# Turning the memory's P on VectorE and moving it through DRAM, with a new order in GpSimd's queue

## The chip, the cores and the metric

The kernel runs on one core of a Trainium2 chip. The metric is the device time of one execution in microseconds; the median of three runs is given. A profile of one execution shows each engine's instructions (PE = TensorE, with PEld for its weight loads, DVE = VectorE, ACT = ScalarE, POOL = GpSimd, SP = SyncE) and the DMA traffic.

## The reference, cut to what matters

Two layers of a hybrid decoder trunk: sequence 256, model width 1024, all in f32.

```python
for l in range(2):
    h = rms_norm(x, norm_g[l])
    q_a, k_a, v_a, q_h, f_h, i_h, q_m, z = split(h @ w_in[l], 512-wide columns)   # z is 1536 wide
    o_a = causal softmax attention, 8 heads x 64 (256 keys are one block: only the own block counts)
    o_h = rms_norm(hgrn2 recurrence, 4 heads x 128)
    km, vm = split(rms_norm(mem, mem_norm_g[l]) @ w_mem_kv[l])                     # 256 memory tokens
    p   = softmax(norm(q_m) @ norm(km).T * 128**-0.5)                              # 4 heads x 128
    o_m = p @ vm
    y = concat(o_a, o_h, o_m) * silu(z)
    x = x + y @ w_out[l]
```

The softmax weights p of the memory attention are "the memory's P" below; those of the causal attention are "the first P" (heads 0 to 3) and "the second P" (heads 4 to 7). The gated output of the recurrence, before it is turned, is "zh".

## The kernel before, in words

**Weights in chunks.** PE is fed by weights of 128 x 1024 f32 (512 KB). For each layer 60 chunks pass in order: 8 of w_mem_kv, 40 of w_in (four for each 512-wide group of columns, the last four groups being QM, VA, ZA, ZM), and 12 of w_out. Each matmul product is made from split operands: a high half (`wh`, made by ACT at L186 or L189) and the rest (`wl`, by DVE at L198 or L201), and three matmuls for each product. SP loads the raw chunk (`wr`, four buffers, L161); there are three buffers each for `wh` and `wl`. A chunk's high half is traced three chunks ahead of its use, the low half two, the load five.

**Generators.** Everything else (norms, attention, the recurrence) is written as generators. `slot()` is called twice for each chunk (L231), and each call lets every active generator go one step; `yield n` waits n steps. `st["c"]` counts the chunks done. `done` holds names that generators wait for. This fixes the order in which instructions are traced. A scheduler then orders each engine's instructions by its own simulation of time, so an instruction that it holds to be ready can overtake an earlier one. `tc.keep_in_program_order(ins)` ties an instruction behind the one traced just before it on the same engine; `mm_row` is a matmul tied in this way; `tc.issue_after(ins)` ties what is issued in its block behind `ins` on that engine.

**Turning a tile.** To turn a 128-row tile there are two ways. On PE: transposes against `ident` into PSUM, then copies to SBUF. Or `across` (L88): DVE transposes 32 x 32 blocks into `blk` (L95), one DMA writes `blk` to the DRAM tile `there` (L103), and four DMAs, one for each strip of 32 rows, read it back in the turned order (L108). `kn` and `kr` go this way on SP's queue; the first P, the second P and zh go this way on GpSimd's queue. `there` has two buffers.

**The end of a layer.** In time order: the first P is turned (into the tile `PT`), the memory's queries are turned on PE (L1068), the memory's scores (L1087 ff.), their softmax (L1100 to L1118), the transposes of the memory's P on PE (L1128, eight for each of two units, with two copies on ACT and two subtractions on DVE into the two halves of the tile `mP`), then P·V of the first P (L1015, L1016) and of the memory (L1142). Then comes w_out (L1164), which takes its 12 row blocks in the order recurrence, causal attention, memory (`KT_ORDER`). Its first four blocks need zh turned and split (`unstripped`, L122: `yh` by ACT at L125, `yl` by DVE at L126); the branch outputs of the attentions are split in `y_store` (L742). zh is sent on its way after the second P has been turned by DVE (`y_turned`, L752).

Of the kernel before, what the change touches and what calls it, by code (L numbers as in the profile page):

```python
# [3 lines left out]

# [8 lines left out]
F32 = mybir.dt.float32  # L13
F32R = mybir.dt.float32r
# [4 lines left out]
OP = mybir.AluOpType  # L19
# [26 lines left out]
def hymba_kernel(ctx: ExitStack, tc: tile.TileContext, x, mem, mem_t, positions, w_in, w_out, w_mem_kv,  # L46
                 gains, moba_g, out):
    nc = tc.nc
    cst = ctx.enter_context(tc.tile_pool(name="cst", bufs=1))
    sb = ctx.enter_context(tc.tile_pool(name="sb", bufs=1))  # L50
    psum = ctx.enter_context(tc.tile_pool(name="psum", bufs=1, space=PS))
    away = ctx.enter_context(tc.tile_pool(name="away", bufs=1, space=bass.MemoryType.DRAM))
# [8 lines left out]
    held = {"sd": 0, "P": 0, "PTh": 0, "PTl": 0, "blk": 0}  # L61
    room_of = {"sd": 4, "P": 2, "PTh": 1, "PTl": 1, "blk": 1}

    def room(what, n=1):
        while held[what] + n > room_of[what]:
            yield
# [9 lines left out]
    def side_tile():  # L76
        held["sd"] += 1
        assert held["sd"] <= 4
        return psum.tile([128, 512], F32, name="sd", tag="sd", bufs=4)

    def rel(what="sd", n=1):
        held[what] -= n
# [2 lines left out]
        return sb.tile([128, n], F32, name=name, tag=name, bufs=2)  # L85


    def across(dst, src, n, stage=None, free=None, name=None, q=None):  # L88
        q = q or nc.sync
        if stage is None:  # L90
            yield from room("blk")
            held["blk"] += 1
        tag = stage or "blk"
        blk = sb.tile([128, 4, n * 32], F32, name="blk", tag=tag, bufs=1)
        nc.vector.transpose(blk.rearrange("p c (n i) -> p c n i", n=n),  # L95
                            src.rearrange("p (n c i) -> p c n i", n=n, c=4))
        if free is not None:
            rel(free)
        if name is not None:
            done.add(name)  # L100
        yield 2
        there = away.tile([4, 32, 4, n * 32], F32, name="there", tag="there", bufs=2)
        q.dma_start(there.rearrange("q j c r -> (q j) c r"), blk)  # L103
        if stage is None:
            rel("blk")
        yield 4
        for c in range(4):
            q.dma_start(dst[c * 32:c * 32 + 32], there[:, :, c].rearrange("q j r -> j q r"))  # L108
            if c == 1:
                yield  # L110

    def turned(a, stage=None, q=None):
        yield from across(a.rearrange("p (q r) -> p q r", q=4), a, 8, stage, q=q)
        yield 5

    def strips(a):
# [2 lines left out]
    def strip_of(o, t):  # L119
        return o[:, :, t * 128:(t + 1) * 128].rearrange("p h (q i) -> p h q i", q=4)  # L120

    def unstripped(oh, ol, a):  # L122
        for t in range(2):
            src, to = strips(a)[:, :, t], strip_of(oh, t)
            nc.scalar.copy(to, src)  # L125
            nc.vector.tensor_tensor(strip_of(ol, t), src, to.bitcast(F32), op=OP.subtract)  # L126

    chunks = []

# [28 lines left out]
    st = {"dma": 0, "h": 0, "l": 0, "c": 0}  # L158
# [51 lines left out]
    T = {}  # L210

    def step():
        for e in list(active):
            e[0] -= 1
            if e[0] <= 0:
                try:
                    e[0] = next(e[1]) or 1
                except StopIteration:
                    active.remove(e)
# [11 lines left out]
    def slot(first):  # L231
        if first:
            c = st["c"]
            dma_to(c + 1 + DMA_AHEAD)
            h_to(c + 1 + H_AHEAD)
            l_to(c + 1 + L_AHEAD)
        step()

    def mm(o, a, b, s, e):
        nc.tensor.matmul(o, lhsT=a, rhs=b, start=s, stop=e)  # L240
# [347 lines left out]
    def heads(t, n):  # L588
        return t.rearrange("p (h d) -> p h d", h=n)
# [161 lines left out]

    def y_turned(l):  # L752
        flat = zh.rearrange("p t s -> p (t s)")
        while f"turned1{l}" not in done:
            yield
        yield from turned(flat, "hq0", nc.gpsimd)
        unstripped(*y_tiles(H_), flat)
        yield
        for k in range(4):
            done.add(f"y{4 * H_ + k}_{l}")  # L760
# [213 lines left out]
    def g_moba_unit(l, u, P, mx):  # L974
        rq, nr = T["rq"], T["nr"]
        nb = small("nba%d" % u, 8)
        sm = small("sma%d" % u, 8)
        ri = small("ria%d" % u, 8)
        if u:
            yield from room("sd", 2)  # L980
            ps = second(u)
            yield
            second_masked(u, ps, P, mx)
        nc.vector.tensor_tensor(nb.rearrange("p (t h) -> p t h", t=2), mx.rearrange("p (t h) -> p t h", t=2),  # L984
                                nr.rearrange("p (t h) -> p t h", t=2)[:, :, 4 * u:4 * u + 4], op=OP.mult)
        yield
        for t in range(2):
            for i in range(4):
                c, r = t * 4 + i, t * 8 + 4 * u + i
                nc.scalar.activation(P[:, i, kc[t]], P[:, i, kc[t]], AF.Exp, bias=nb[:, c:c + 1],  # L990
                                     scale=rq[:, r:r + 1], accum_out=sm[:, c:c + 1])
            yield
        yield
        nc.vector.reciprocal(ri, sm)
        for t in range(2):
            for i in range(4):
                c = t * 4 + i
                nc.vector.tensor_scalar(P[:, i, kc[t]], P[:, i, kc[t]], ri[:, c:c + 1], None, op0=OP.mult)
        yield 2
        tag = ("PTh", "PTl")[u]  # L1000
        yield from take(tag)
        PT = sb.tile([128, 4, 384], F32, name="PT", tag=tag, bufs=1)
        yield from across(PT, P.rearrange("p i s -> p (i s)"), 12, free="P", name=f"turned{u}{l}", q=nc.gpsimd)
        yield 13
        while f"va{l}" not in done or f"z{A_}{l}" not in done:
            yield
        va = T["va"]
        yield from room("sd")
        po = side_tile()
        for i in range(4):  # L1010
            h = 4 * u + i
            rows, c = slice(64 * (i % 2), 64 * (i % 2) + 64), (i // 2) * 256
            pieces = PT.rearrange("p q (n s) -> p n q s", n=12)[:, 3 * i:3 * i + 3]
            o = po[rows, c:c + 256].rearrange("p (b q s) -> p b q s", b=2, q=4)
            (mm if i else mm_row)(o, va[:, 0, h * 64:(h + 1) * 64], pieces[:, 0:2], True, False)  # L1015
            mm(o[:, 1], va[:, 1, h * 64:(h + 1) * 64], pieces[:, 2], False, True)  # L1016
        rel(tag)
        yield
        y_store(l, A_, u, po)
# [58 lines left out]
    def g_mem_unit(l, u, qm, r, nr):  # L1078
# [36 lines left out]
        for t in range(2):  # L1115
            for i in range(2):
                c = 2 * t + i
                nc.vector.tensor_scalar(P[:, t, i], P[:, t, i], ri[:, c:c + 1], None, op0=OP.mult)  # L1118
        yield 5
        while f"scores1{l}" not in done:  # L1120
            yield
        PT = [sb.tile([128, 2, 2, 256], F32R, name="mP", tag=n, bufs=1) for n in (("hF", "kmh"), ("ih", "kml"))[u]]
        for b in range(2):
            yield from room("sd")
            pt = side_tile()
            for i in range(2):
                for t in range(2):
                    nc.tensor.transpose(pt[:, i * 256 + t * 128:i * 256 + (t + 1) * 128],  # L1128
                                        P[:, t, i, b * 128:(b + 1) * 128], ident)
            nc.scalar.copy(PT[0][:, b], heads(pt, 2))  # L1130
            nc.vector.tensor_tensor(PT[1][:, b], heads(pt, 2), PT[0][:, b].bitcast(F32), op=OP.subtract)
            rel()
        if u == 0:
            rel("P")
        yield 8
        yield from room("sd")
        po = side_tile()
        for i in range(2):
            hs = slice((2 * u + i) * 128, (2 * u + i + 1) * 128)
            for b in range(2):  # L1140
                for x, y in passes:
                    (mm if i or b or x != passes[0][0] or y != passes[0][1] else mm_row)(po[:, i * 256:(i + 1) * 256], vm[x][:, b, hs], PT[y][:, b, i],  # L1142
                       b == 0 and (x, y) == passes[0], b == 1 and (x, y) == passes[2])
        yield
        while f"z{M_}{l}" not in done:
            yield
        y_store(l, M_, u, po)
# [2 lines left out]
    def w_out_phase(l):  # L1150
# [6 lines left out]
        def part(i, n, kt, t, cols=(0, 1), o=0, w=512, pinned=False, to=None):  # L1157
            br, k = divmod(kt, 4)
            yh, yl = (a[:, k, t * 128:(t + 1) * 128] for a in T[f"y{br}"])
            for c in cols:  # L1160
                cs = slice(c * 512 + o, c * 512 + o + w)
                a = acc[t][c][:, o:o + w] if to is None else to[:, :w]
                for j, (y, wt) in enumerate(((yh, whs[i]), (yh, wls[i]), (yl, whs[i]))):
                    ins = nc.tensor.matmul(a, lhsT=y, rhs=wt[:, cs], start=n == (0 if to is None else nk - 2) and j == 0,  # L1164
                                           stop=n == nk - 1 and j == 2)
                    if pinned:
                        tc.keep_in_program_order(ins)

        def fin():
# [108 lines left out]
```

## Time and profile before

| | |
|---|---|
| median of 3 runs | 397.27 us (395.93, 397.27, 397.28) |
| the profiled execution's own time | 399.69 us |
| its span in the profile | 397.9 us |
| PE busy | 390.5 us, 2871 matmuls |
| DVE, ACT, POOL busy | 314.6, 251.1, 70.3 us |
| bytes moved by DMA | 80.33 MB, 202 GB/s over the span |
| of these on GpSimd's queue | 8.39 MB |

The span is the time between the first and the last instruction in the profile; the execution's own time has a little more around it. The chain that ended last is followed back from the last instruction, at each step to what released it. A windows view gives each engine's busy time in a stretch of the span, the TensorE clock that was granted (1.00 is full) and the mean busy share of the 16 DMA engines. Layer 0's last stretch lies at about 128 to 198 us, layer 1's at about 320 to 394 us.

### The profile page before, as it was taken

Reading aid. Unit: us, or ns where it says so; the run is one execution under the profiler, and the core shown is the slowest. Engines: PE = TensorE matmul, PEld = TensorE weight load, DVE = VectorE, ACT = ScalarE, POOL = GpSimd, SP = SyncE. Lnnn points to the kernel's source line nnn. Section 1 sums busy time; section 2 is a strip of 40 time slices with the busy share of each in tenths; the row PEclk is TensorE's granted clock in tenths of the full one; section 3 lists DMA queues with packets and bytes.
Section 4 is the critical chain, followed back from the end, with each engine's and each line's share of the span. In section 5 each row is a group of like instructions: output and inputs, shape, how many; then the busy total and the mean of one; then the engine's idle time right before and its main releaser. Section 6 shows DMA issues by size and latency. Waiting matters only on the chain.

```text
span 397.9 us, 7596 instructions
## 1 busy us (share of the span) xinstructions
PE 390.5 (98%) x2871; PEld 326.1 (82%) x2871; DVE 314.6 (79%) x606; ACT 251.1 (63%) x422; POOL 70.3 (18%) x109
## 2 busy tenths in 40 slices
PE   8999999999999999999999999999999999979996
PEld 5888888878788888788888888887888789867885
DVE  4789999889759998964576889799965999766743
ACT  5998746557778669544466766546856884954440
POOL 2013401604103432000000040050330061400000
PEclk9999999999999999999999999999999999999999
DMA  8986794377634989546565469637943398981612
GB/s 267 411 294 213 245 244 158 100 259 218 202 110 152 238 308 263 205 122 219 188 202 169 164 215 238 234 107 226 249 163 107 105 281 271 270 236 55 203 61 105
DMA packets 24901, 80.33 MB, mean 202 GB/s; under 512 B 3233, under 2 KB 5665, under 8 KB 24865
## 3 DMA queue, kind: packets, MB, share of 16 engines
q1 hardware_dynamic: 22304, 71.31, 56.0%
q0 software_dynamic: 2272, 8.39, 7.9%
q8 instruction: 22, 0.36, 0.4%
q10 hardware_dynamic: 288, 0.15, 0.1%
q14 instruction: 15, 0.11, 0.1%
HBM read 72.51 MB, written 7.34 MB: 201 GB/s over the span
## 4 chain that ended last, share of the span: by engine, by line
PE 86%; DMA 4%; DVE 4%; POOL 2%; issue 2%; ACT 1%; SPq 0%; ACTq 0%; DVEq 0%; POOLq 0%
PE acc L240 58%; PE acc L1164 17%; PE sd L240 5%; PE sd L244 3%; DMA zh<-there 3%; DMA wr<-in_w_mem_kv_dram 1%; DVE wl L198 1%; PE sd L453 1%; ACT wh L186 1%; POOL rka L904 1%; POOL PT L108 0%; PE sd L1068 0%; PE sd L939 0%; PE sd L1128 0%; POOL rtB L548 0%
## 5 line engine op out<-in xcount | busy, mean ns | idle before, releaser
L198 DVE TENSOR_TENSOR wl<-wr,wh 128x1024 fp32r<-128x1024 f32 x96 | 116.8, 1219 | 39.4 <-ACT wh L186 39.3
L186 ACT CAST wh<-wr 128x1024 fp32r<-128x1024 f32 x96 | 100.6, 1050 | 67.0 <-PE acc L240 45.2
L240 PE MATMUL acc<-wh,hT 128*128 128x512 f32 x384 | 124.8, 396 | 0.0
L240 PEld LDWEIGHTS acc<-wh,hT 128*128 128x128 f32 x384 | 71.8, 188 | 16.1 <-issue 0.7
L240 PE MATMUL acc<-wl,hT 128*128 128x512 f32 x192 | 75.2, 392 | 0.0
L240 PE MATMUL acc<-hT,wh 128*128 128x512 f32 x256 | 65.2, 393 | 0.0
L240 PEld LDWEIGHTS acc<-hT,wh 128*128 128x128 f32 x256 | 45.9, 189 | 8.2 <-ACT kn L607 0.4
L240 PEld LDWEIGHTS acc<-wl,hT 128*128 128x128 f32 x192 | 36.1, 188 | 7.0 <-DVE wl L198 0.2
L201 DVE SCALAR_TENSOR_TENSOR wl<-wr,gT,wh 128x1024 fp32r<-128x1024 f32 (+1 forms) x29 | 31.2, 1097 | 12.4 <-ACT wh L189 12.1
L189 ACT ACTIVATE wh<-wr,gT 128x1024 fp32r<-128x1024 f32 (+1 forms) x29 | 28.6, 1002 | 16.5 <-PE acc L1164 8.2
L1164 PE MATMUL acc<-wl,yh 128*128 128x512 f32 (+1 forms) x96 | 37.7, 392 | 0.0
L240 PEld LDWEIGHTS acc<-hT,wl 128*128 128x128 f32 x256 | 35.2, 190 | 2.5
L1164 PE MATMUL acc<-wh,yl 128*128 128x512 f32 (+1 forms) x96 | 37.1, 392 | 0.0
L240 PE MATMUL acc<-hT,wl 128*128 128x256 f32 x256 | 36.6, 283 | 0.0
L1164 PE MATMUL acc<-wh,yh 128*128 128x512 f32 (+1 forms) x96 | 30.4, 396 | 2.0 <-ACT yh L125 2.0
L240 PE MATMUL acc<-wh,mTh 128*128 128x512 f32 x64 | 25.1, 395 | 0.5 <-DVE mTh L392 0.3
L240 PE MATMUL acc<-wh,mTl 128*128 128x512 f32 x64 | 24.8, 390 | 0.0
L1164 PEld LDWEIGHTS acc<-wh,yh 128*128 128x128 f32 x96 | 18.3, 190 | 6.1 <-ACT yh L125 2.2
L990 ACT ACTIVATE P<-P,nba,rq 128x128 f32<-128x128 f32 (+1 forms) x32 | 17.1, 535 | 8.3 <-DVE nba L984 8.3
L1164 PEld LDWEIGHTS acc<-wh,yl 128*128 128x128 f32 x96 | 18.3, 191 | 3.8
L1164 PEld LDWEIGHTS acc<-wl,yh 128*128 128x128 f32 x96 | 18.3, 191 | 3.6
L240 PE MATMUL acc<-wl,mTh 128*128 128x512 f32 x64 | 20.2, 392 | 0.0
(222 smaller groups left out, 575.0 us busy)
## 6 DMA issues: line engine op xcount, KB each, us to landing
wr<-in_w_in_dram SPq DMA_DIRECT2D x80, 512.0 KB, 4.2
wr<-in_w_out_dram SPq DMA_DIRECT2D x24, 512.0 KB, 5.1
wr<-in_w_mem_kv_dram SPq DMA_DIRECT2D x15, 512.0 KB, 4.4
there<-blk POOLq DMA_DIRECT2D x4, 768.0 KB, 4.2
PT<-there POOLq DMA_DIRECT2D x16, 192.0 KB, 6.9
there<-blk SPq DMA_DIRECT2D x4, 512.0 KB, 3.6
xs<-in_x_dram SPq DMA_DIRECT2D x2, 512.0 KB, 8.8
memr<-in_mem_dram SPq DMA_DIRECT2D x2, 512.0 KB, 6.7
```

The costliest lines, as they stand in the source:

```text
L186: nc.scalar.copy(whs[i], raws[i])
L189: nc.scalar.activation(whs[i][:, sl], raws[i][:, sl], AF.Copy, scale=gT[:, g:g + 1])
L198: nc.vector.tensor_tensor(wls[i], raws[i], whs[i].bitcast(F32), op=OP.subtract)
L201: ins = nc.vector.scalar_tensor_tensor(wls[i][:, sl], in0=raws[i][:, sl], scalar=gT[:, g:g + 1], in1=whs[i][:, sl].bitcast(F32), op0=OP.mu ...
L240: nc.tensor.matmul(o, lhsT=a, rhs=b, start=s, stop=e)
L244: tc.keep_in_program_order(nc.tensor.matmul(o, lhsT=a, rhs=b, start=s, stop=e))
L453: ins = nc.tensor.transpose(pt[:, j * 256 + t * 128:j * 256 + (t + 1) * 128], xn[t][:, k * 128:(k + 1) * 128], ident)
L904: nc.gpsimd.tensor_tensor(r[:, t8], ms[:, t8], pw[:, :8], op=OP.pow)
L990: nc.scalar.activation(P[:, i, kc[t]], P[:, i, kc[t]], AF.Exp, bias=nb[:, c:c + 1], scale=rq[:, r:r + 1], accum_out=sm[:, c:c + 1])
L1164: ins = nc.tensor.matmul(a, lhsT=y, rhs=wt[:, cs], start=n == (0 if to is None else nk - 2) and j == 0, stop=n == nk - 1 and j == 2)
```

## The change

- The memory's P (two units `u`, two heads each) is no longer turned on PE. DVE turns its 32 x 32 blocks into a `blk`, GpSimd's queue writes both units to DRAM and reads each back in four strips, into the tile P itself. One copy on ACT and one subtraction on DVE, each over 1024 columns from SBUF, make the two halves `mP`. The P·V matmuls read the turned tile with an access pattern of runs of 32 (`cols`).
- GpSimd's queue gets an order by `issue_after` and by names in `done`: first P, zh, second P, the memory's two units. In program order zh waits for the first P's strips to be issued, in place of the second P's turn on DVE.
- The strips are issued in the order 0, 2, 1, 3, and `there` has five buffers.
- The split of zh, and the memory's split, are tied in program order, and traced at fixed chunks: `reach(l, 46)` for zh, 51 and 52 for the memory's two units. P·V of the first and second P are traced at chunk 47 and 50. Chunk 48 is the first of w_out.
- The memory's P·V now comes among w_out's chunks; the first matmul of w_out traced after it is tied behind it.

```diff
-    def across(dst, src, n, stage=None, free=None, name=None, q=None):
+    def across(dst, src, n, stage=None, free=None, name=None, q=None, behind=None):
...
         yield 2
-        there = away.tile([4, 32, 4, n * 32], F32, name="there", tag="there", bufs=2)
-        q.dma_start(there.rearrange("q j c r -> (q j) c r"), blk)
+        while behind is not None and behind not in done:
+            yield
+        there = away.tile([4, 32, 4, n * 32], F32, name="there", tag="there", bufs=5)
+        with tc.issue_after(T[behind].ins) if behind is not None else nullcontext():
+            q.dma_start(there.rearrange("q j c r -> (q j) c r"), blk)
...
-        for c in range(4):
-            q.dma_start(dst[c * 32:c * 32 + 32], there[:, :, c].rearrange("q j r -> j q r"))
-            if c == 1:
+        for c in (0, 2, 1, 3):
+            ins = q.dma_start(dst[c * 32:c * 32 + 32], there[:, :, c].rearrange("q j r -> j q r"))
+            if c == 2:
                 yield
+        if name is not None:
+            T[name + "moved"] = ins
+            done.add(name + "moved")
...
-            nc.scalar.copy(to, src)
-            nc.vector.tensor_tensor(strip_of(ol, t), src, to.bitcast(F32), op=OP.subtract)
+            tc.keep_in_program_order(nc.scalar.copy(to, src))
+            tc.keep_in_program_order(nc.vector.tensor_tensor(strip_of(ol, t), src, to.bitcast(F32), op=OP.subtract))
...
+    def reach(l, c):
+        while st["c"] < 60 * l + c:
+            yield
...
     def y_turned(l):
-        while f"turned1{l}" not in done:
+        while f"turned0{l}moved" not in done:
             yield
-        yield from turned(flat, "hq0", nc.gpsimd)
+        yield from turned(flat, "hq0", nc.gpsimd, f"zh{l}")
+        yield from reach(l, 46)
         unstripped(*y_tiles(H_), flat)
...
-        yield from across(PT, P.rearrange("p i s -> p (i s)"), 12, free="P", name=f"turned{u}{l}", q=nc.gpsimd)
-        yield 13
+        yield from across(PT, P.rearrange("p i s -> p (i s)"), 12, free="P", name=f"turned{u}{l}", q=nc.gpsimd,
+                          behind=f"zh{l}moved" if u else None)
+        yield from reach(l, (47, 50)[u])
...
-        yield 5
+        flat = P.rearrange("p t i s -> p (t i s)")
         while f"scores1{l}" not in done:
             yield
-        PT = [sb.tile([128, 2, 2, 256], F32R, name="mP", tag=n, bufs=1) for n in (("hF", "kmh"), ("ih", "kml"))[u]]
-        for b in range(2):
-            yield from room("sd")
-            pt = side_tile()
-            for i in range(2):
-                for t in range(2):
-                    nc.tensor.transpose(pt[:, i * 256 + t * 128:i * 256 + (t + 1) * 128],
-                                        P[:, t, i, b * 128:(b + 1) * 128], ident)
-            nc.scalar.copy(PT[0][:, b], heads(pt, 2))
-            nc.vector.tensor_tensor(PT[1][:, b], heads(pt, 2), PT[0][:, b].bitcast(F32), op=OP.subtract)
-            rel()
+        blk = sb.tile([128, 4, 256], F32, name="blk", tag=("ih", "kml")[u], bufs=1)
+        nc.vector.transpose(blk.rearrange("p c (n i) -> p c n i", n=8),
+                            flat.rearrange("p (n c i) -> p c n i", n=8, c=4))
+        T[f"mem{u}"] = blk, flat.rearrange("p (q r) -> p q r", q=4)
+        done.add(f"mem{u}{l}")
+        if u:
+            while not {f"turned1{l}moved", f"mem0{l}"} <= done:
+                yield
+            pairs = [T[f"mem{v}"] for v in range(2)]
+            theres = [away.tile([4, 32, 4, 256], F32, name="there", tag="there", bufs=5) for _ in range(2)]
+            last = T[f"turned1{l}moved"]
+            for (b, _), there in zip(pairs, theres):
+                with tc.issue_after(last.ins):
+                    last = nc.gpsimd.dma_start(there.rearrange("q j c r -> (q j) c r"), b)
+            yield 2
+            for (_, d), there in zip(pairs, theres):
+                with tc.issue_after(last.ins):
+                    for c in (0, 2, 1, 3):
+                        ins = nc.gpsimd.dma_start(d[c * 32:c * 32 + 32], there[:, :, c].rearrange("q j r -> j q r"))
+                last = ins
+                yield
+            done.add(f"memmoved{l}")
+        while f"memmoved{l}" not in done:
+            yield
+        yield from reach(l, (51, 52)[u])
+        yield
+        PT = [sb.tile([128, 1024], F32R, name="mP", tag=n, bufs=1) for n in (("hF", "kmh"), ("ih", "kml"))[u]]
+        tc.keep_in_program_order(nc.scalar.copy(PT[0], flat))
+        tc.keep_in_program_order(nc.vector.tensor_tensor(PT[1], flat, PT[0].bitcast(F32), op=OP.subtract))
+        cols = [a.rearrange("p (q t n b s) -> p n b t q s", q=4, t=2, n=2, b=2) for a in PT]
...
+                        po[:, i * 256:(i + 1) * 256].rearrange("p (t q s) -> p t q s", t=2, q=4),
+                        vm[x][:, b, hs], cols[y][:, i, b], b == 0 and (x, y) == passes[0], b == 1 and (x, y) == passes[2])
+        T["held"] = True
...
-                    if pinned:
+                    if pinned or T.pop("held", False):
                         tc.keep_in_program_order(ins)
```

More of the change, by code (lines that the diff above doesn't have):

```diff
@@ L1 @@
 import math
-from contextlib import ExitStack
+from contextlib import ExitStack, nullcontext
 from fractions import Fraction
@@ L106, in across, with turned @@
         yield 4
-        for c in range(4):
-            q.dma_start(dst[c * 32:c * 32 + 32], there[:, :, c].rearrange("q j r -> j q r"))
-            if c == 1:
+        for c in (0, 2, 1, 3):
+            ins = q.dma_start(dst[c * 32:c * 32 + 32], there[:, :, c].rearrange("q j r -> j q r"))
+            if c == 2:
                 yield
-    def turned(a, stage=None, q=None):
-        yield from across(a.rearrange("p (q r) -> p q r", q=4), a, 8, stage, q=q)
+        if name is not None:
+            T[name + "moved"] = ins
+            done.add(name + "moved")
+    def turned(a, stage=None, q=None, name=None):
+        yield from across(a.rearrange("p (q r) -> p q r", q=4), a, 8, stage, q=q, name=name)
         yield 5
@@ L1134, in g_mem_unit @@
             rel("P")
-        yield 8
+        yield 2
         yield from room("sd")
@@ L1141, in g_mem_unit @@
                 for x, y in passes:
-                    (mm if i or b or x != passes[0][0] or y != passes[0][1] else mm_row)(po[:, i * 256:(i + 1) * 256], vm[x][:, b, hs], PT[y][:, b, i],
-                       b == 0 and (x, y) == passes[0], b == 1 and (x, y) == passes[2])
-        yield
+                    (mm if i or b or (x, y) != passes[0] else mm_row)(
+                        po[:, i * 256:(i + 1) * 256].rearrange("p (t q s) -> p t q s", t=2, q=4),
+                        vm[x][:, b, hs], cols[y][:, i, b], b == 0 and (x, y) == passes[0], b == 1 and (x, y) == passes[2])
+        T["held"] = True
         while f"z{M_}{l}" not in done:
```

## The prediction

> **What bounds the kernel now.** I read the page from the top: busy shares, then the chain that ended last, then the timeline of PE where that chain leaves PE.
>
> ```profile
> PE 390.5 (98%) x2871; PEld 326.1 (82%) x2871; DVE 314.6 (79%) x606; ACT 251.1 (63%) x422; POOL 70.3 (18%) x109
> ```
>
> PE is busy 98% of the span. So a microsecond taken off PE's own stream is a microsecond of the kernel, unless a wait takes its place; POOL, at 18%, has room. The chain in order of time shows the two places that the change touches.
>
> ```profile
> 153.18 0.87 PE sd L1128 x8
> ...
> 171.17 1.32 PE sd L240 x11
> 172.49 25.87 PE acc L1164 x114
> ...
> 345.52 10.21 DMA zh<-there
> ```
>
> The first row is one half of layer 0's PE transposes of the memory's P: eight in 0.87 us, so 1.74 us for a layer's 16. The second is one P·V of the memory, all but its first matmul: 12 x 0.12 = 1.44 us. The third gives the pace of w_out's matmuls, 25.87 / 114 = 0.227 us. The last is the fourth strip of zh in layer 1, moved back from DRAM: the chain hangs for 10.21 us on one transfer. The timeline of PE says what that costs.
>
> ```profile
> 153.02 1.04 PE L1128 MATMUL sd<-ident,P 128*128 128x128 f32 x8
> ...
> 172.33 0.40 PE L1164 MATMUL acc<-wh,yh 128*128 128x512 f32 x1
> ...
> 345.04 1.03 PE L1128 MATMUL sd<-ident,P 128*128 128x128 f32 x8
> ...
> 356.51 0.79 PE L1164 MATMUL acc<-wh,yh 128*128 128x512 f32 x1 [2.01 <-ACT yh L125]
> ...
> 368.10 0.40 PE L1164 MATMUL acc<-wh,yh 128*128 128x512 f32 x1
> ```
>
> The same work lies between the same two points of both layers. From the first transposes to the matmul after the memory's second P·V it takes 172.33 - 153.02 = 19.31 us in layer 0, and 368.10 - 345.04 = 23.06 us in layer 1: 3.75 us more. 2.01 us of that is PE idle before 356.51, waiting for the split of zh (yh, L125). The other 1.74 us is clock, as the windows show (columns: window, length, busy time of PE, PEld, DVE, ACT, POOL, then granted clock, DMA share, GB/s).
>
> ```profile
> 348.00:352.00 4.00, 4.00 (x30) 3.42 (x29) 4.00 (x6) 3.21 (x6) 0.00 (x0) 1.00 1.03 227
> 352.00:356.00 4.00, 2.50 (x24) 2.08 (x20) 1.43 (x3) 0.16 (x1) 0.00 (x0) 1.00 0.98 333
> 356.00:360.00 4.00, 3.49 (x10) 2.27 (x12) 3.51 (x6) 3.69 (x7) 0.00 (x0) 0.57 0.08 34
> 360.00:364.00 4.00, 4.00 (x29) 3.22 (x24) 4.00 (x8) 1.85 (x3) 0.00 (x0) 1.00 0.38 131
> 364.00:368.00 4.00, 4.00 (x25) 3.53 (x24) 0.44 (x1) 1.14 (x1) 0.00 (x0) 1.00 0.02 4
> ```
>
> After the wait the granted clock is 0.57 for 4 us: 0.43 x 4 = 1.72 us, which is the missing 1.74. A stall here costs nearly twice its length. The Trainium skill's page "TensorE: Matmul & The Clock Gate", section "HAM oscillation — how this bites in real kernels", warns of PE-idle gaps over about 3.4 us; by that threshold alone a gap of 2.01 us would keep its clock, and the term below would be 2.01. The trace disagrees: 2.01 us of idle was enough.
>
> **The change part by part.** First, the 32 PE transposes go (16 in a layer): 1.74 x 2 = 3.48 us off PE. The second layer's are counted like the first's; their rows have the same length (1.04 and 1.03 for the first eight). I take all of it, since PE is the bound in both places. The P·V matmuls stay, 24 in a layer. Only their moving operand is now read in runs of 32 elements, as the key strips of the memory scores already are.
>
> ```profile
> L240 PE MATMUL sd<-kml,qmh x16: 281/283/285, 132.2 to 330.9; 128*128 128x256 f32 x16
> L240 PE MATMUL sd<-mP,vml x16: 277/283/283, 161.0 to 367.9; 128*128 128x256 f32 x16
> ```
>
> Strips and whole rows both have a median of 283 ns, so nothing is added there.
>
> Second, zh moves ahead of the second P in POOL's queue. Now, in layer 1 (DVE and POOL, in order of time):
>
> ```profile
> 323.27 1.25 DVE L95 STREAM_TRANSPOSE blk<-zh 128x1024 f32<-128x1024 f32 x1
> 325.95 0.31 POOL L1059 TENSOR_SCALAR nrm<-qmr 128x8 f32<-128x8 f32 x1
> 333.03 1.20 POOL L103 DMA_DIRECT2D there<-blk  x2 [6.77 <-DVE blk L95]
> 338.11 2.25 POOL L108 DMA_DIRECT2D PT<-there  x4 [3.88 <-PE acc L240]
> 345.52 0.55 POOL L108 DMA_DIRECT2D zh<-there  x1 [3.17 <-issue]
> ```
>
> zh is turned at 324.5, yet it leaves only after the second P at 333.6, and its last strip is held to 345.5. In the new order it leaves when POOL is free, at 326.3 (nothing but DMAs follows on POOL in this layer, so no arithmetic is queued behind zh's wait). The write out takes 6.6 us (row below), four issues 2.25 us, a strip 13.1 us: landed by 326.3 + 6.6 + 2.25 + 13.1 = 348.3 where now it is 345.52 + 10.21 = 355.7. The second P leaves after zh's issues, at 335 in place of 333; its P·V is held to the end of the second w_out chunk, about 356, so 2 us are covered there.
>
> ```profile
> there<-blk POOLq DMA_DIRECT2D x1, 512.0 KB, 6.6
> zh<-there POOLq DMA_DIRECT2D x3, 128.0 KB, 13.1
> ```
>
> What is late next is the split itself. PE was ready for w_out at 356.51 - 2.01 = 354.5; without the transposes, and with the memory's first P·V no longer before it, it is there at 354.5 - 1.74 - 1.44 = 351.3. The copy of zh is held behind the weight split of the second w_out chunk.
>
> ```profile
> 349.07 1.18 ACT L189 ACTIVATE wh<-wr,gT 128x1024 fp32r<-128x1024 f32 x1
> 355.84 1.14 ACT L125 CAST yh<-zh 128x512 fp32r<-128x512 f32 x2 [4.63 <-DMA zh<-there]
> ```
>
> That split ends at 350.25 and the first copy, half of 1.14, at 350.8: 0.5 us ahead of PE. The cover is thin, and if zh came later than 350, the wait would be back. Behind the copy on ACT stands the next weight's split, which PE needs two chunks (5.4 us) later. I charge 0.5 us a layer for it, between nothing and 1.3 (the DVE half of the split behind one more 1.25 us instruction). So the 3.75 us come back in the profiled execution, less 0.5 in each layer.
>
> Third, DVE and ACT. For a layer DVE gains two transposes of 1.25 us (as zh's above) and exchanges four subtractions from PSUM for two of twice the width; ACT likewise with its copies (its share in 348 to 352 is 3.21 of 4).
>
> ```profile
> L1131 DVE TENSOR_TENSOR mP<-sd,mP x8: 681/682/686, 157.7 to 352.7; 128x512 fp32r<-128x512 f32 x8
> L198 DVE TENSOR_TENSOR wl<-wr,wh 128x1024 fp32r<-128x1024 f32 x96 | 116.8, 1219 | 39.4 <-ACT wh L186 39.3
> ```
>
> DVE: 2 x 1.25 + 2 x 1.22 - 4 x 0.68 = +2.2 us a layer. The 2.7 us that go end at 353, after four full microseconds of DVE; the subtractions come back after 364, where DVE is busy 0.44 us of 4. The transposes fall behind the normalising of P (next fence), around 345. I cost this at nothing beyond the 0.5 above; if a weight's low half is pushed late by one of them, it is up to 1.25 us.
>
> ```profile
> 343.49 1.14 DVE L1118 TENSOR_SCALAR P<-P,rim 128x256 f32<-128x256 f32 x4
> ```
>
> Fourth, the memory's P by DRAM: per layer two writes of 512 KB and eight reads of 128 KB, ten more issues on POOL at 0.55 (5.5 us, POOL is idle) and 2 MB on the DMA engines. P is normalised at 344.6 and turned by 346; out 346 to 353; the eight reads issue from 353 in 8 x 0.55 + a hold like the 3.17 us above, so to 361. The row nearest to them is a strip of zh at 10.2 to 13.1 us under full engines; with the share at 0.38 and less after 360 I take 3 to 7. The first copy of it is held behind the weight split that waits for the fourth w_out chunk: 351.3 + 48 x 0.227 + 1.5 (the second P's P·V, taken like the memory's 1.44) = 363.7, plus about 1.1 for that split = 364.8; the second one chunk and one P·V on, 368.9. Behind it stands the split of a weight that PE needs three chunks later. w_out takes the memory's rows last. The first P's strips, issued by 355, then land by 362, the second's by 368: nothing lies on the path. Bounds: nothing, or, at 13.1 us a strip, 355 + 13.1 - 364.8 = 3.3 us late.
>
> **Sum.** Profiled execution: 399.69 - 3.48 - 3.75 + 1.0 = 393.5. Its time is 2.42 above the median of 397.27, so part of its wait may be its own; the fastest of the three, 395.93, is 3.76 lower, just the price of the wait. So the median run contains between 1.34 (397.27 - 395.93) and 3.75 us of it; the middle, 2.5, is my choice, with no row to prefer an end. 397.27 - 3.48 - 2.5 + 1.0 = 392.3. Ends: 390.0 with all 3.75 and no new wait, 394.9 with 1.34 and 1.3 a layer.
>
> **Rivals.** (1) Weights come late. The DMA engines are full from 340 to 356 (share 1.03 at 348), and 2.1 MB more at 280 GB/s (the mean of 227 and 333 in the full windows) are 7.5 us of them, about half before 356. The third w_out chunk was asked for at 340.1 and landed 13.6 us later:
>
> ```profile
> 340.10 0.33 SPq L161 DMA_DIRECT2D wr<-in_w_out_dram  x1
> wr<-in_w_out_dram SPq DMA_DIRECT2D x1, 512.0 KB, 13.6
> ```
>
> At 353.7, plus 1.18 and 1.22 for the splits, it is ready at 356.1 against a need at 351.3 + 5.4 + 1.5 = 358.2. 2 us of slack against 2 to 4 us of new traffic, less the 1 MB of zh that moves ahead of 348. If a weight is 1 us too late in each layer, with or without a part of the clock loss: 392.3 + 2.0 to 3.2 = 394.3 to 395.5.
>
> (2) Slower: the memory's strips miss the copy that waits for them in order. From 364.8 on each microsecond idles PE, for the next w_out matmul is held behind the P·V, and a 2 us gap brings the clock loss of 1.74. At 13.1 us a strip (3.3 us late, some 2 of them not filled by other matmuls, an assumption) that is 3.7 us a layer, 7.5 in both, against a gain of 6.0: 398.8 by this sum, and over 399.3 if 2.3 us a layer are not filled. It decides from 1.3 us of unfilled wait in each layer. For it: the strips are last in POOL's queue and POOL's issues are held. Against: the share is 0.02 to 0.38 after 360. The Trainium skill's "SBUF — State Buffer", section "SBUF: two separate sides", says that a DVE instruction in a two-port mode locks GpSimd out while it writes a DMA's descriptors, which would stretch the issues under a busy DVE; here the four of 338.11 took 2.25 us, 0.56 each, and the one of 345.52 0.55, on either side of DVE's full stretch; no run here shows more.
>
> (3) Little comes of it: PE's 3.48 us are spent waiting for ACT and DVE, busy 3.21 and 4.00 us of the 4 from 348, and of the wait for zh only its lower price returns, less the 0.5 in each layer: 397.27 - 1.34 + 1.0 = 396.9. Against it: PE waits for neither of them there now.
>
> **How the numbers follow.** Forecast 0.57 (own range 390.0 to 394.9), rival 1 0.17, rival 3 0.13, rival 2 0.13. The measurement tells about 0.5%, 2 us: below 395.3 lie the forecast and most of rival 1, 0.73; within are rival 3 and the mild end of rival 2, 0.15; slower 0.12. The range goes from 389.7, just under the low end, to about rival 3's 396.9.
>
> **What would show it.** No rows of L1128; the PE wait for yh in layer 1 gone and no clock below 0.9 in w_out; zh landed before 348 in both layers; the memory's strips landed before 365; no wait of ACT for wr. Wrong if PE waits at the memory's P·V or in w_out's first four chunks.

## The result, and the profile after

The changed kernel takes 400.88 us, the median of four runs (400.60 to 401.16), against 397.12 for the kernel before: a ratio of 1.0096, 95% interval 1.0072 to 1.0119. It is slower by 1%, where 392.3 was forecast. The execution shown below took 401.16 us, with a span of 399.4.

The busy shares, as quoted of before:

```profile
PE 388.8 (97%) x2839; PEld 320.9 (80%) x2839; DVE 318.8 (80%) x606; ACT 250.0 (63%) x418; POOL 81.5 (20%) x129
```

PE runs 32 matmuls fewer (2839 for 2871): the transposes are gone. Yet its share fell from 98% to 97%, so it now waits for something. The waits say for what (us in total, times, longest):

```profile
PE acc L1196 <- ACT wh L192: 2.3, 2, 1.1
PE acc L1196 <- DVE as L334: 2.0, 2, 1.0
...
PE acc L1196 <- DVE wl L204: 0.6, 2, 0.3
```

Three waits, all in w_out (L1196), each twice, so once in a layer. The wait for zh's `yh`, the only one that w_out had before, is no longer in this list. The windows put the new ones in time (columns as in the prediction; layer 0):

```profile
156.00:160.00 4.00, 4.00 (x28) 3.37 (x24) 4.00 (x7) 3.71 (x7) 0.55 (x1) 1.00 1.01 349
160.00:164.00 4.00, 3.01 (x13) 2.08 (x12) 4.00 (x6) 1.69 (x4) 2.23 (x4) 1.00 0.93 300
...
180.00:184.00 4.00, 2.87 (x17) 1.95 (x15) 1.65 (x2) 2.03 (x3) 0.00 (x0) 1.00 0.00 0
184.00:188.00 4.00, 3.63 (x21) 2.94 (x21) 2.18 (x4) 0.48 (x1) 0.00 (x0) 1.00 0.42 133
```

One hole lies at the start of w_out, with DVE full; another 20 us later, with DVE, ACT and the DMA engines (share 0.00) all with time to spare. The clock stays at 1.00 in both. PE's timeline has the instructions:

```profile
160.24 0.40 PE L1196 MATMUL acc<-wl,yh 128*128 128x512 f32 x1
161.62 0.47 PE L1196 MATMUL acc<-wh,yh 128*128 128x512 f32 x1 [0.99 <-DVE as L334]
...
173.52 0.84 PE L1196 MATMUL acc<-wh,yh 128*128 128x512 f32 x3
...
175.56 0.84 PE L1196 MATMUL acc<-wh,yh 128*128 128x512 f32 x3
...
177.60 0.84 PE L1196 MATMUL acc<-wh,yh 128*128 128x512 f32 x3
...
179.64 0.28 PE L254 MATMUL sd<-mP,vmh 128*128 128x256 f32 x1
...
183.07 0.97 PE L1196 MATMUL acc<-wh,yh 128*128 128x512 f32 x3 [1.14 <-ACT wh L192]
184.33 0.50 PE L1196 MATMUL acc<-wl,yh 128*128 128x512 f32 x1 [0.29 <-DVE wl L204]
186.07 0.39 PE L254 MATMUL sd<-mP,vmh 128*128 128x256 f32 x1
```

The two rows of `mP` are the starts of the memory's two P·V, and neither has a wait. The hole sits between them, ahead of a split weight.

The idle time in brackets is less than a wait costs. PE starts a matmul of w_out every 0.23 us and each row is 0.39 us long or more, so the rows overlap. The wait of 0.99 us puts 1.38 us between two starts (160.24 and 161.62), which is 1.15 lost. The length of the whole stage is the better measure: from w_out's first matmul to the first of the next stage, layer 0 takes 41.49 us here (159.54 to 201.03). The runs below are compared by it.

ACT's timeline around the hole:

```profile
173.76 1.05 ACT L192 CAST wh<-wr 128x1024 fp32r<-128x1024 f32 x1 [1.18 <-PE acc L1196]
174.72 1.04 ACT L1161 CAST mP<-P 128x1024 fp32r<-128x1024 f32 x1
181.97 1.04 ACT L192 CAST wh<-wr 128x1024 fp32r<-128x1024 f32 x1 [6.21 <-PE acc L1196]
```

The copy of the memory's first P (L1161) waits for no transfer. But the next split of a weight waits 6.21 us for PE, and then PE waits for it: a ring of `wh` buffers in which none is free. The order in which PE's instructions stand in the compiled program, in w_out's chunks 0 to 11 and its four accumulators 0 to 3, shows why (P.V is P·V):

```
chunk 3: 0 1 2 3 | chunk 4: 0 1 3 | chunk 5: 0 1 3 | chunk 6: 0 1 3 | first P.V of the memory
chunk 4: 2 | chunk 7: 0 1 3 | second P.V of the memory | chunk 5: 2 | chunk 6: 2 | chunk 7: 2 | chunk 8: 0 1 2 3
```

The timeline agrees in its counts: the rows of three at 173.52, 175.56 and 177.60 are each followed by six single matmuls, so nine matmuls for each of three chunks, where a whole chunk has twelve. `T["held"]` ties one matmul, the first of chunk 4 for accumulator 2, behind the P·V. The scheduler put the P·V late, and filled the time with the other three accumulators of chunks 4, 5 and 6. So three chunks were each left with three matmuls to do, and three chunks are all the buffers there are.

### The profile page after: what moved, and what is told of

Same layout as the page of the kernel before. It is cut to its first block, busy times and chain, and to the rows that moved or that the text cites. A ratio compares the mean times of both kernels' runs of the same rounds, so it can differ in the third digit from the quotient of the medians.

```text
span 399.4 us, 7566 instructions
## 1 busy us (share of the span) xinstructions
PE 388.8 (97%) x2839; PEld 320.9 (80%) x2839; DVE 318.8 (80%) x606; ACT 250.0 (63%) x418; POOL 81.5 (20%) x129
## 4 chain that ended last, share of the span: by engine, by line
PE 78%; DVE 6%; ACT 6%; DMA 4%; issue 3%; POOL 2%; SPq 0%; ACTq 0%; DVEq 0%; POOLq 0%
PE acc L250 55%; PE acc L1196 14%; PE sd L250 4%; PE sd L254 3%; ACT P L1119 2%; DMA there<-blk 2%; ACT wh L192 2%; DVE wl L204 2%; DMA wr<-in_w_mem_kv_dram 2%; PE sd L463 1%; DVE wl L207 1%; POOL PT L111 1%; POOL rka L915 1%; ACT mP L1161 0%; PE sd L950 0%
## 5 line engine op out<-in xcount | busy, mean ns | idle before, releaser
L1196 PE MATMUL acc<-wl,yh 128*128 128x512 f32 (+1 forms) x96 | 37.7, 393 | 0.7 <-DVE wl L204 0.6
L1196 PE MATMUL acc<-wh,yl 128*128 128x512 f32 (+1 forms) x96 | 37.0, 389 | 0.0
L1196 PE MATMUL acc<-wh,yh 128*128 128x512 f32 (+1 forms) x96 | 32.2, 397 | 4.2 <-ACT wh L192 2.3
L250 PE MATMUL acc<-hT,wl 128*128 128x256 f32 x256 | 35.7, 282 | 0.0
L1196 PEld LDWEIGHTS acc<-wh,yh 128*128 128x128 f32 x96 | 17.7, 188 | 9.8 <-ACT wh L192 3.6
L1196 PEld LDWEIGHTS acc<-wl,yh 128*128 128x128 f32 x96 | 18.0, 188 | 5.7 <-DVE wl L204 2.5
L1196 PEld LDWEIGHTS acc<-wh,yl 128*128 128x128 f32 x96 | 17.9, 188 | 3.9 <-DVE yl L132 0.5
```

## The experiments

Theory 1: the pin holds the buffers. Theory 2: at w_out's start PE now arrives before DVE and ACT have emptied the accumulators of the last group of w_in, and this carries the loss. Theory 3: a transfer is late (strips or weights).

**A fourth `wh` buffer, pin kept.**

```diff
-RAW_BUFS, WH_BUFS, WL_BUFS = 4, 3, 3
+RAW_BUFS, WH_BUFS, WL_BUFS = 4, 4, 3
```

> The changed kernel with four buffers instead of three for the high halves of the weights (wh); nothing else. Theory 1 (the pin holds buffers: one matmul of w_out is tied behind the memory's first P.V, PE's order lets the other accumulators overtake it, three chunks stay unfinished and all three wh buffers stay taken, so ScalarE's split of the fourth waits 6.2 us and PE waits for it, about 2.5 us a layer): the fourth buffer lets that split run, ScalarE's idle time of 6.2 us ends on something else, and most of the 2.5 us a layer goes, about 397 us. The third low half (wl) is still held, so 0.3 to 0.6 a layer may stay. Theory 2 (PE waits at the start of w_out for an accumulator that VectorE's sum frees, 1.15 us a layer, and that is the larger loss): that wait stays, and the time is within 0.5 of 400.9. Theory 3 (the transfers are late: strips or weights): no change, 400.9.

394.49 us (393.00 to 395.94); ratio to before 0.9939 (0.9911 to 0.9968), 6.4 us under the changed kernel. All of PE's waits in this profile:

```profile
PE sd L250 <- DVE dm L378: 1.0, 1, 1.0
PE acc L250 <- ACT wh L195: 0.7, 1, 0.7
PE sd L254 <- DVE mP L1162: 0.7, 2, 0.3
```

The three waits of w_out are gone; 0.35 us a layer for the second `mP` is new. Theory 3 falls here: 6.4 us came back with no transfer changed in kind or order, and in the changed kernel none of ACT's waits in w_out ends on a strip or on the load of a w_out weight. Two points of the expectation were wrong. The time is 2.5 us under the 397 expected. And ACT's 6.21 us did not end on something else. It is still there, ACT's timeline:

```profile
179.83 1.06 ACT L192 CAST wh<-wr 128x1024 fp32r<-128x1024 f32 x1 [6.21 <-PE acc L1196]
```

With four buffers it is the split of the next chunk that waits, and PE has a whole chunk of work in hand meanwhile. The idle time of an engine off the path is no measure of the loss: the same 6.21 us go with 1.43 us of PE's idle time a layer in one kernel, and in the other with the 0.35 for the second `mP` alone, whose copy stands behind this split on ACT (at 181.31). That the wait at the start went too was not expected, and because of it this run does not tell theories 1 and 2 apart; the runs below do.

**No pin, and the memory's P·V traced earlier.**

```diff
-        yield from reach(l, (51, 52)[u])
+        yield from reach(l, (49, 50)[u])
...
-        T["held"] = True
```

> The changed kernel without the pin behind the memory's P.V, and with the memory's P.V released at w_out's chunks 1 and 2 instead of 3 and 4, which in PE's order puts both P.V together after chunk 5, all chunks whole. Theory 1: ScalarE's 6.2 us and PE's waits of 1.14 and 0.29 at the weights' splits go, 2.5 us a layer: 400.9 - 5.0 = about 395.9. Theory 2: the start wait of about 1.0 a layer stays, so that the time stays near 400.9 if it carries the loss. Theory 3: with the P.V earlier the strips have less time; PE waits at the first P.V, and the time is above 401.

395.22 us (394.62 to 395.75); ratio 0.9951 (0.9930 to 0.9973). The two lines together were worth 400.88 - 395.22 = 5.66 us, 2.8 a layer, where 5.0 was expected. Layer 0's w_out says the same: 38.68 us (159.27 to 197.95) in place of 41.49, so 2.81 less. PE's waits in w_out: of the three rows, one is left, and it stands as it was.

```profile
PE acc L1195 <- DVE as L334: 2.0, 2, 1.0
```

This separates theories 1 and 2: the held buffers cost 5.7 and the start, so far, an idle time of 2.0. The copies of the memory's P ran 2.5 and 10 us earlier here (both from 172.25, where the changed kernel has 174.72 and 183.44), and no wait for strips appeared.

**No pin, nothing else.** The edit is the last line of the one above alone.

> The changed kernel without the pin behind the memory's P.V, and nothing else. PE's order then has whole chunks, the first P.V after chunk 6 and the second just ahead of the last two blocks of matmuls. Theory 1: the 2.5 us a layer at the splits go; the second half of the memory's y comes late instead (0.7 sum, 0.6 copy, 0.7 rest behind the last P.V, against 3 us of matmuls that stand between), so 396 to 398. Theory 2: 400.9, with the start wait as it was. Theory 3: 400.9 or less.

402.35 us (401.47 to 403.97), ratio 1.0136 (1.0090 to 1.0182): slower than the changed kernel, and a miss by 4 to 6 us. The waits at the splits are gone, as theory 1 has it. But with nothing to tie it the second P·V slid to the end of w_out, where its result is needed at once. PE's waits, then its timeline and windows:

```profile
PE acc L1195 <- ACT yh L756: 3.8, 2, 2.4
PE acc L1195 <- DVE as L334: 2.0, 2, 1.0
```

```profile
193.77 0.28 PE L250 MATMUL sd<-mP,vmh 128*128 128x256 f32 x1
196.46 0.50 PE L1195 MATMUL acc<-wh,yh 128*128 128x512 f32 x1 [2.41 <-ACT yh L756]
...
197.78 0.63 PE L1195 MATMUL acc<-wh,yh 128*128 128x512 f32 x1
```

```profile
192.00:196.00 4.00, 2.05 (x15) 1.76 (x13) 2.16 (x3) 1.36 (x2) 0.00 (x0) 1.00 0.57 194
196.00:200.00 4.00, 3.54 (x9) 2.53 (x10) 1.38 (x2) 0.41 (x1) 0.00 (x0) 0.63 0.43 131
```

My expectation had counted 3 us of matmuls between the last P·V and the need for it; there were none. And after the gap of 2.41 us the clock is down to 0.63 in the mean of four us, and matmuls took 0.63 us where they take 0.39. So some pin, or an earlier place, was needed: what was wrong was a pin on one matmul of a group whose others could pass it. The 5.66 us are the price of the held buffers, then, and not what it gains to drop the pin alone. The earlier place with the pin kept was not run.

**All of the change but the memory's part.** TensorE turns the memory's P again, with the old P·V and no pin; GpSimd's queue, the zh split and the five far buffers stay as changed.

> The changed kernel with the memory's tail as it was before (TensorE turns the P, 32 transposes; P.V at its old place; no pin), and with all the rest of the change: GpSimd's queue holds first P, zh, second P, the splits of zh in program order, five buffers for the far side. Theories 1 and 2 (all that was lost hangs on the memory's part): as before, less the wait for zh in layer 1, which is 3.75 us in the profiled execution of before and taken as 1.3 to 2.5 in its median run: 394.6 to 395.8 us, no wait of ScalarE of 6 us, no wait for the accumulator at w_out's start. Theory 3 (the new order of the queue makes weights or P late): 397 or more, with PE waiting for the second P's P.V or for weights.

396.17 us (395.75 to 396.81), ratio 0.9978 (0.9956 to 1.0000): 0.8 us under before, 0.4 above the expected stretch. PE has no wait in w_out at all, so the zh move does what it says. But it brings 0.8 us in the medians, where I had taken 2.5; by the interval it is between nothing and 1.7. In the profiled executions the spans differ by 397.9 - 394.4 = 3.5, so the wait of 3.75 was real there. That most executions of the kernel before hold less of it is what the medians suggest; no second trace of that kernel shows it.

**The start of w_out.** Three runs. First, other ready matmuls put in PE's way, in the version of 395.22:

```diff
...
+        lead = [(0, c, j) for c in range(2) for j in range(2)] + [(1, c, j) for j in range(2) for c in range(2)]
+        for n, c, j in lead:
+            yh = T[f"y{H_}"][0][:, n, 0:128]
+            w = (whs, wls)[j][c0 + n]
+            tc.keep_in_program_order(nc.tensor.matmul(acc[0][c], lhsT=yh, rhs=w[:, c * 512:c * 512 + 512],
+                                                      start=n == 0 and j == 0, stop=False))
...
```

These are matmuls of chunks 0 and 1 for the first two accumulators, tied in this order. The loop that follows leaves them out, and its first matmul for the third accumulator is tied behind them.

> The version with both P.V together after chunk 5 and no pin (measured 395.22), and in w_out's start the high-half matmuls of the second chunk for the first two accumulators tied ahead of the third accumulator's first matmul. Theory 2 (the 1.0 us a layer at w_out's start is PE standing before an accumulator that VectorE's sum has not freed, so other ready work in front covers it): four matmuls at 0.23 us stand in the gap, the wait falls from 1.0 to 0.3 or less a layer, 393.6 to 394.0. If what is late there is the whole input (the low half of zh, the weights' low half), the wait only moves to those: 395.2.

394.47 us (394.25 to 395.05), ratio 0.9951 (0.9936 to 0.9965). The wait changed as theory 2 says:

```profile
PE acc L1197 <- DVE yl L132: 0.4, 2, 0.2
```

1.0 a layer became 0.2, now for zh's low half. PE is busy 3.67 of the four us from 160 in place of 2.98. But the time fell by 0.75 only, and not at all in the ratios to before. The trace says why it is little: layer 0's w_out takes 38.22 us (159.39 to 197.61) in place of 38.68. In front of the accumulator stands now a weight's low half, whose matmuls start at 161.07 when DVE has made it (159.74 + 1.27 = 161.01), and behind it zh's low half, at 162.00. So both forecasts hold in part: the matmuls cover the wait for the sum, and PE meets the next things that DVE has to make.

Second, DVE's turn of the second P behind the sums, in the changed kernel with its pin:

```diff
+        if u:
+            yield from reach(l, 48)
+            yield
...
+        if u:
+            tc.keep_in_program_order(ins)
```

The last sums of ZM, the last group of w_in, are tied in order likewise.

> The changed kernel (pin kept) with VectorE's turn of the memory's second P tied behind the last sums of w_in's last group, so that 1.24 us of VectorE's work stands behind the sums instead of ahead. Theory 2, VectorE's queue being what is late: PE's wait for the sum at w_out's start (1.0 us a layer) falls to 0.4 or less, and the time by 1 to 2 us, 399 to 400. If ScalarE's copy of the accumulator ahead of the sum is as late (it ran at 160.8, with ScalarE busy from 158.2): the wait stays at 0.7 to 1.0 and the time at 400.9. The strips of the memory leave 7 us later, and may make PE wait at the first P.V; that would be slower than 401.

400.36 us (400.06 to 402.23), ratio 1.0109 (1.0080 to 1.0138). The wait halved and changed its owner:

```profile
PE acc L1203 <- ACT yh L758: 1.0, 2, 0.5
```

Moving 1.24 us of DVE work gained 0.5 us of PE's time a layer, and then ACT was what is late: neither of the two forecasts whole. At that place both engines are full, and taking load off one exposes the other. In the time it is half a us, less than the run resolves.

Third, the fourth buffer in the version of 395.22, the pin gone.

> The same version (395.22) with four wh buffers. Theory 1: the buffers are no longer held, so the fourth gives nothing at the splits. What it gave beside that, with the pin, was the wait at w_out's start (1.0 us a layer, gone in that trace, since the splits of w_out's first chunks run earlier and VectorE's sum comes at 159.5 instead of 161.1): 395.22 - 2.0 = about 393.2. If the fourth buffer gave only the release of held buffers: 395.2.

392.33 us (392.01 to 394.85), ratio 0.9905 (0.9882 to 0.9929): faster than before by 0.95%, and than the changed kernel by 8.5 us (7.6 by the ratios to before). The buffer brings 2.9 us in the medians and 1.8 by the ratios, where 2.0 was expected and nothing is held any more; the two versions stand beside different runs of before, with medians of 396.98 and 396.60. The traces lie between: layer 0's w_out falls from 38.68 to 37.32 us (159.19 to 196.51), 2.7 for two layers. All of PE's waits:

```profile
PE sd L250 <- DVE dm L378: 1.0, 1, 1.0
PE acc L250 <- ACT wh L195: 0.8, 2, 0.4
PE acc L250 <- DVE mTh L402: 0.4, 1, 0.4
```

None lies in w_out. How a weight's buffer cures a wait for an accumulator is on DVE's timeline, first of the changed kernel, then of this one:

```profile
159.87 1.27 DVE L207 SCALAR_TENSOR_TENSOR wl<-wr,gT,wh 128x1024 fp32r<-128x1024 f32 x1
161.06 0.42 DVE L334 TENSOR_TENSOR as<-acc,al 128x256 f32<-128x256 f32 x1
```

```profile
156.60 1.24 DVE L207 SCALAR_TENSOR_TENSOR wl<-wr,gT,wh 128x1024 fp32r<-128x1024 f32 x1
...
159.35 0.41 DVE L334 TENSOR_TENSOR as<-acc,al 128x256 f32<-128x256 f32 x1
```

The high half of that weight is split earlier (on ACT at 152.83, in the changed kernel at 156.49), so its low half is too, and the sum that stood behind it comes 1.7 us sooner: PE's wait of 0.99 us is covered.

**The control: the kernel before with four `wh` buffers.**

> Control: the kernel before with four wh buffers. Theory 1: no buffer is held there and PE has no wait for a split in w_out, so no change beyond 0.5 us: 396.5 to 397.5. If the fourth buffer is worth several us by itself, whatever the pin (rival): 393 to 395.

396.68 us (395.63 to 397.26), ratio 0.9986 (0.9957 to 1.0014): no change, as theory 1 has it. PE has no wait in w_out in this trace. The buffer is worth something only where the change made PE wait for what it frees.

## Why the prediction was wrong

**The transposes, 3.48 us: right.** Their rows are gone. The best version stands 392.33 against 396.60 for the runs of before beside it, 4.27 less, and 3.48 + 0.8 of the zh move are 4.28. That they agree to 0.01 is luck: by the interval the gain is 2.8 to 4.7 us. Rival 3, by which these 3.48 us were spent waiting for ACT and DVE, came true in part: the wait at w_out's start is such a wait, for DVE, and took 2.7 us in the changed kernel. It is not the whole story, for the version without that wait gets the gain back.

**The zh move, 2.5 us in the median: right in its mechanism, mis-sized.** It measured 0.8, below my lower end of 1.34. That end was the distance from the median of three runs to the fastest of them, 397.27 - 395.93; over 25 later runs it is 396.98 - 395.68 = 1.30, so the runs were not too few. But a kernel without the wait has such a distance too, 396.17 - 395.75 = 0.42 in the run above, and only the rest can be the wait's. In layer 1 zh's strips were issued later than I worked out (335.69 instead of 332.9) and landed earlier, by 335.69 + 2.22 + 3.6 = 341.5, since a strip took 3.6 us and not 13.1:

```profile
335.69 2.22 POOL L111 DMA_DIRECT2D zh<-there  x4 [5.87 <-DMA there<-blk]
...
354.55 2.24 POOL L1152 DMA_DIRECT2D P<-there  x4 [2.20 <-DMA there<-blk]
357.40 1.66 POOL L1152 DMA_DIRECT2D P<-there  x3 [0.61 <-issue]
360.30 0.56 POOL L1152 DMA_DIRECT2D P<-there  x1 [1.24 <-issue]
```

**"What is late next is the split itself", 0.5 us a layer: the wrong instruction, and less than half the price.** I saw that PE would reach w_out 3.2 us earlier, and looked only at what its first matmul reads. The fifth in PE's order writes an accumulator that had to be emptied first, by a copy on ACT and a sum on DVE. In the kernel before, the P·V and the transposes covered these: in layer 0 that sum started at 161.32, against 161.06 after, but w_out started at 162.31, against 159.54. An operand has a producer, but a destination has a last reader, and I did not look for it. It is 0.99 us of idle time a layer, 1.36 by w_out's length. My term for DVE has a part in it. I put DVE's two turns of the memory's P at around 345 and their cost at nothing; the second ran at 350.15, inside the full stretch of DVE ahead of the sum, and the run that moved it behind the sums took 0.5 us off the wait.

**"Nothing lies on the path" of the memory's strips: true, and the wrong question.** This is the step that failed, and it carries the sign. The strips were in time (layer 1): the first unit's by about 354.55 + 2.24 + 7.3 = 364.1 (7.3 us is the median from issue to landing of these eight), the second's by some 368, and the copies ran at 369.21 and 377.93, waiting for no transfer. I had quoted the rule that the next w_out matmul is held behind the P·V, but priced it only for strips that miss (rival 2). In truth the tie acts with the strips in time, because it fixes one matmul and leaves the scheduler free to pass it with others, each of which keeps a weight's buffer. That is 5.66 us, which stood in no term; the sum had nothing in its place. My sign of being wrong, a wait in w_out's first four chunks, did appear, but it is the other fault, the start. Rival 2 had the right place and the wrong cause: late data, for which it needed 1.3 us a layer. Rival 1 (weights late from memory) did not occur: ACT waited for no raw weight of w_out. As for DVE holding up POOL's issues, the two rows cited in rival 2 both lie ahead of DVE's full stretch from 348, not on either side of it. The changed kernel shows what they were to show: the seven issues from 354.55 to 359.06 took 0.55 to 0.56 us each, with DVE busy 9.90 of the ten us from 350.

Put together in medians: 397.12 - 3.48 - 0.8 + 2.9 (the start) + 5.66 (the held buffers) = 401.4, against 400.88 measured. This sum tests little: 2.9 and 5.66 are themselves differences between the measured versions, and the 0.5 us left are what the median of before differs by (397.12 and 396.60). What stands apart from it is w_out's length. Against the forecast of 392.3 it gives 2 x 2.81 for the held buffers and 2 x 1.36 - 1.0 for the start, and the zh move lacks 2.5 - 0.8: 9.0 us, against the 8.6 by which the forecast was missed. My upper end of 394.9 was also added up 0.15 too low: its terms give 395.05.

## What to carry to other kernels

When work in front of a phase is taken away, list for its first instructions not only who writes what they read, but who last reads what they write, and how busy those engines are there. And before a tie is put on one instruction, ask what may pass it and what each that passes keeps in its hands: with three buffers, three unfinished chunks stop the pipeline, though no data are late. A wait of 6 us on an engine beside the path proves nothing by itself; it took a fourth buffer, the same version without the tie, and the same buffer in the kernel before to tell which wait carried the time.

## What the runs showed of the hardware

After an idle gap of 2.01 us on PE (the kernel before) and of 2.41 us (the run without the pin) the granted clock fell. A narrow window shows 0.50 both times, from 356.42 to 359.82 and from 197.01 to 200.41, so about 3.4 us at half clock and 1.7 us lost, though one gap was longer; the 0.57 and 0.63 above are means over four us. After gaps of 0.99 and 1.14 us (the changed kernel), and of 1.43 and 1.64 us (the run without the pin, before 391.36 and 8.24), it stayed at 1.00. So in these runs the limit lies between 1.64 and 2.01 us, below the roughly 3.4 us of the Trainium skill's "TensorE: Matmul & The Clock Gate", section "HAM oscillation — how this bites in real kernels". Whether the length of the gap alone decides, no run here shows.

In layer 1 the same 128 KB strips from DRAM on GpSimd's queue took 13.1 us (median) from issue to landing behind the second P in the kernel before, and 3.6 (zh) and 7.3 us (the memory's P) here; a strip's time from one place in the queue is no price for another.
